# Scaling a pooled result run in two 16 KB halves instead of in one 32 KB piece

## The chip, the core and the metric

The kernel runs on one core of one Trainium2 chip. The metric is the device time of one execution in microseconds (us); less is better. The kernel before took 1569.69 us, the median of 3 runs (1565.55 to 1570.47).

## What is computed

The reference is an average pool over the last axis with window 4 and stride 4, so the windows do not overlap:

```python
x = randn(64, 256, 8192) in float32; kernel_size = stride = 4
for i in range(out_len):                      # out_len = 2048
    output[:, :, i] = mean(x[:, :, 4*i : 4*i + 4], axis=2)
```

Every output element is the sum of four neighbouring inputs, times 1/4. The input has 536.87 MB and the output 134.22 MB, and each byte crosses between HBM and SBUF once.

## The kernel before, in words

As a window never crosses a row, the whole input is treated as one long array. It is cut into 64 blocks of 128 partitions x 16384 floats (64 KB in each partition, 8 MB in all). Two consecutive blocks (k = 0 and k = 1) make a run, so there are 32 runs. A block gives 4096 results in each partition (16 KB), and a run gives 8192 (32 KB in each partition, 4 MB in all). There are two input buffers, `xt[0]` for every k = 0 block and `xt[1]` for every k = 1 block, and two result buffers, `ot[0]` and `ot[1]`, which alternate from run to run (`q`).

Four engines have fixed parts:

- SyncE (SP) issues the loads of 8 MB (`load`, line 63). It waits until VectorE has finished with a buffer (semaphore `free`, line 89) and at once issues the load of the next run's block into that buffer (`ahead`, line 92).
- VectorE (DVE) waits for a loaded block (`full[k]`, line 85), and ahead of a run's first block also for the store that last read this result buffer (`stored[q]`, line 87). Then it sums neighbours twice (`sums`): line 76 adds the even and odd elements of the block in place (16384 to 8192), and line 78 adds again into the half of `ot[q]` that belongs to the block (8192 to 4096).
- ScalarE (ACT) multiplies by 1/4 in place (line 95). SP tells it by the semaphore `summed` (line 91) that the sums are there.
- The store of 4 MB (line 97) is issued by ACT itself, after it has waited for its own multiplication (`scaled`). In the last run but one SP issues it, and waits for `scaled_last`.

The order of work is written out by hand with semaphores: `take(engine, sem, n)` (lines 59 to 60) makes an engine wait for a count and takes it off again, so all waits stand on line 60 in the profile. The function `pair` (lines 82 to 97) does one run. A loop of 15 iterations with two runs each covers runs 0 to 29 (line 119); run 30 stands by itself behind it (line 122) and issues the loads of the last run, whose k = 1 block is cut into two pieces (lines 112 to 113). Run 31 is written out in lines 126 to 141: it already scales its first half and its two quarter pieces separately, and ACT issues its stores of 3 MB and 1 MB.

Loads all go into SP's DMA queue, and the stores of runs 0 to 29 and 31 into ACT's. Both queues are served by the same 16 DMA engines.

Of the kernel before, what the change touches and what calls it, by code (L numbers as in the profile page):

```python
# [1 line left out]

# [4 lines left out]


FULL = 16384
PAIR = 2  # L10
ROUND = 2 * PAIR

TAIL = (8192, 8192)


@with_exitstack
def kernel(
    ctx: ExitStack,
    tc: tile.TileContext,
    x: bass.AP,  # L20
    kernel_size: bass.AP,
    stride: bass.AP,
    out: bass.AP,
):
    nc = tc.nc
    K, S = int(kernel_size), int(stride)
    assert K == S == 4
    B, C, L = x.shape
    assert L % K == 0
    P = nc.NUM_PARTITIONS  # L30
    dt = x.dtype
    add, mult = mybir.AluOpType.add, mybir.AluOpType.mult

    M = FULL // K
    blocks = B * C * L // P // FULL
    runs = blocks // PAIR
    assert blocks * P * FULL == B * C * L and blocks % ROUND == 0 and sum(TAIL) == FULL

    xr = x.rearrange("b c l -> (b c l)").rearrange("(n p k m) -> n k p m", p=P, k=PAIR, m=FULL)
    orun = out.rearrange("b c l -> (b c l)").rearrange("(n p m) -> n p m", p=P, m=PAIR * M)  # L40


    xt0 = ctx.enter_context(nc.sbuf_tensor([P, FULL], dt))
    xt1 = ctx.enter_context(nc.sbuf_tensor([P, FULL], dt))
    ot0 = ctx.enter_context(nc.sbuf_tensor([P, PAIR * M], dt))
    ot1 = ctx.enter_context(nc.sbuf_tensor([P, PAIR * M], dt))
    xt, ot = [xt0, xt1], [ot0, ot1]


    full = [nc.alloc_semaphore(f"full{k}") for k in range(2)]  # L50
    piece = [nc.alloc_semaphore(f"piece{k}") for k in range(len(TAIL))]
    free = nc.alloc_semaphore("free")
    summed = nc.alloc_semaphore("summed")
    summed_last = nc.alloc_semaphore("summed_last")
    scaled = nc.alloc_semaphore("scaled")
    scaled_last = nc.alloc_semaphore("scaled_last")
    stored = [nc.alloc_semaphore(f"stored{k}") for k in range(2)]

    def take(engine, sem, n):
        engine.wait_ge(sem, n).then_inc(sem, -n)  # L60

    def load(n, k):
        d = nc.sync.dma_start(out=xt[k][:, :], in_=xr[n, k])
        d.then_inc(full[k], 16)
        return d

    for k in range(2):
        tc.no_tile_sem_insts.add(load(0, k).ins.name)  # L70
    tc.close()
    tc.compile()  # L72

    def sums(t, o):
        w = t.shape[1]
        nc.vector.tensor_tensor(out=t[:, : w // 2], in0=t[:, ::2], in1=t[:, 1::2], op=add)  # L76
        nc.vector.drain()
        return nc.vector.tensor_tensor(  # L78
            out=o, in0=t[:, : w // 2 : 2], in1=t[:, 1 : w // 2 : 2], op=add
        )  # L80

    def pair(n, q, ahead, store):

        for k in range(PAIR):
            take(nc.vector, full[k], 16)
            if k == 0:
                take(nc.vector, stored[q], 16)
            sums(xt[k][:, :], ot[q][:, k * M : (k + 1) * M]).then_inc(free, 1)
            take(nc.sync, free, 1)
            if k == 1:  # L90
                nc.sync.sem_inc(summed, 1)
            ahead(k)
        done = scaled if store is nc.scalar else scaled_last
        take(nc.scalar, summed, 1)
        nc.scalar.mul(ot[q][:, :], ot[q][:, :], 1.0 / K).then_inc(done, 1)  # L95
        take(store, done, 1)
        store.dma_start(out=orun[n], in_=ot[q][:, :]).then_inc(stored[q], 16)


    zero = nc.const_aps.tensor(0.0, [P, 1], dt)  # L100
    nc.scalar.mul(ot[0][:, :1], zero, 1.0).then_inc(stored[0], 16)  # L101
    nc.scalar.sem_inc(stored[1], 16)

    edges = [sum(TAIL[:i]) for i in range(len(TAIL) + 1)]
    pieces = list(zip(edges[:-1], edges[1:]))
    xe, oe = xr[runs - 1, 1], orun[runs - 1]

    def ahead_of_last(k):
        if k == 0:
            load(runs - 1, 0)  # L110
        else:
            for sem, (a, b) in zip(piece, pieces):
                nc.sync.dma_start(out=xt[1][:, a:b], in_=xe[:, a:b]).then_inc(sem, 16)

    engines = (mybir.EngineType.SP, mybir.EngineType.DVE, mybir.EngineType.Activation)
    with nc.Fori(0, (runs - 2) // 2, 1, engines=engines) as r:
        for q in range(2):
            n = r * 2 + q
            pair(n, q, lambda k: load(n + 1, k), nc.scalar)


    pair(runs - 2, 0, ahead_of_last, nc.sync)

    take(nc.vector, stored[1], 16)
    take(nc.vector, full[0], 16)
    sums(xt[0][:, :], ot[1][:, :M]).then_inc(summed_last, 1)
    for k, (sem, (a, b)) in enumerate(zip(piece, pieces)):
        take(nc.vector, sem, 16)  # L130
        sums(xt[1][:, a:b], ot[1][:, M + a // K : M + b // K]).then_inc(summed_last, 1)
        if k == 0:
            take(nc.scalar, summed_last, 1)
            nc.scalar.mul(ot[1][:, :M], ot[1][:, :M], 1.0 / K)  # L134
        o = ot[1][:, M + a // K : M + b // K]
        take(nc.scalar, summed_last, 1)
        nc.scalar.mul(o, o, 1.0 / K).then_inc(scaled, 1)  # L137
        take(nc.scalar, scaled, 1)
        c = 0 if k == 0 else M + a // K
        d = M + b // K  # L140
        nc.scalar.dma_start(out=oe[:, c:d], in_=ot[1][:, c:d]).then_inc(stored[1], 16)
    take(nc.sync, stored[0], 16)
    take(nc.sync, stored[1], 16 * len(TAIL))


# [1 line left out]
_INS = ['x', 'kernel_size', 'stride']  # L147
_OUTS = [((64, 256, 2048), 'float32')]

_NUMBERS = {'kernel_size': 4, 'stride': 4}  # L150


# [26 lines left out]
```

## Time and profile before

| | |
|---|---|
| median of 3 runs | 1569.69 us |
| the profiled execution | 1568.75 us |
| its span, first to last instruction | 1567.4 us |
| VectorE busy | 839.8 us (54%) |
| ScalarE busy | 226.8 us (14%) |
| bytes through the DMA engines | 671.09 MB, 428 GB/s over the span |
| share of the 16 DMA engines' time, SP's queue q1 and ACT's queue q10 | 80.6% and 19.2% |
| one store of 4 MB from ACT, issue to landing | 33.5 us (median of 30) |
| one load of 8 MB, issue to landing | 35.2 us (median of 63) |

An engine counts as busy only while it computes; waits, semaphore steps and issuing a DMA do not count. A group of the profile stands for the instructions of one line, with their count, their busy time and the mean duration of one; the number behind the bar is the time the engine stood idle just before them, and what ended it. "DVEq L60" as the releaser is the engine's own wait in `take`. The timeline gives each instruction's start, measured from the start of the span.

### The profile page before, as it was taken

The page shows a single profiled execution, that of the slowest core. Times are in us where ns is not written, and L with a number is a line of the kernel's source. Part 1 is how long each engine was busy: PE and PEld are TensorE (multiplying, and loading weights), DVE is VectorE, ACT ScalarE, POOL GpSimd, SP SyncE. Part 2 cuts the span into 40 slices and gives each one's busy share as a digit, 9 for nine tenths or more (in the row PEclk, how much of TensorE's full clock was granted, in tenths as well). Part 3 has the DMA queues.
Part 4 walks back from the last instruction along what each step waited for, and adds up shares of the span by engine and source line. Part 5 has one row for each costly group of instructions (what it writes and reads, how often), then busy time and mean ns, then how long its engine had stood idle before and what let it go on. Part 6 is the DMA issues. An engine that isn't in the chain of part 4 may idle for free. (4 is left out here: it accounts for less than half of the span.)

```text
span 1567.4 us, 935 instructions
## 1 busy us (share of the span) xinstructions
DVE 839.8 (54%) x130; ACT 226.8 (14%) x36; POOL 0.2 (0%) x4
## 2 busy tenths in 40 slices
DVE  3654546545465454654546546465464654646546
ACT  0111011110111101111011110111101111011111
POOL 0000000000000000000000000000000000000000
DMA  9999999999999999999999999999999999999998
GB/s 428 415 428 442 428 421 435 430 426 440 422 439 426 445 426 429 437 420 439 428 426 431 427 436 428 429 426 431 433 423 428 423 427 434 428 429 424 431 429 378
DMA packets 14112, 671.09 MB, mean 428 GB/s; under 512 B 1568, under 2 KB 1568, under 8 KB 1568
## 3 DMA queue, kind: packets, MB, share of 16 engines
q1 hardware_dynamic: 9504, 541.07, 80.6%
q10 hardware_dynamic: 4608, 130.03, 19.2%
HBM read 536.87 MB, written 134.22 MB: 428 GB/s over the span
## 5 line engine op out<-in xcount | busy, mean ns | idle before, releaser
L76 DVE TENSOR_TENSOR xt<-xt 128x8192 f32<-128x8192 f32 (+1 forms) x65 | 556.5, 8561 | 710.2 <-DVEq L60 710.2
L95 ACT ACTIVATE ot<-ot 128x8192 f32<-128x8192 f32 x31 | 217.9, 7029 | 1306.3 <-ACTq L60 1306.3
L78 DVE TENSOR_TENSOR ot<-xt 128x4096 f32<-128x4096 f32 (+1 forms) x65 | 283.4, 4360 | 4.8
L134 ACT ACTIVATE ot<-ot 128x4096 f32<-128x4096 f32 x1 | 3.6, 3617 | 13.4 <-ACTq L60 13.4
L137 ACT ACTIVATE ot<-ot 128x2048 f32<-128x2048 f32 x2 | 3.8, 1910 | 8.0 <-ACTq L60 8.0
L101 ACT ACT_TABLE_LOAD x1 | 1.3, 1283 | 2.4 <-PEq L72 2.4
L101 ACT ACTIVATE ot<-const-float32-0.0 128x1 f32<-128x1 f32 x1 | 0.2, 202 | 0.0
L160 POOL MEMSET const-bfloat16-1.0<- 128x1 bf16 x1 | 0.1, 101 | 0.0
L160 POOL MEMSET const-uint8-127<- 128x1 uint8 x1 | 0.1, 101 | 0.0
L160 POOL MEMSET const-float32-0.0<- 128x1 f32 x1 | 0.1, 98 | 0.2 <-issue 0.2
L160 POOL MEMSET const-float32-1.0<- 128x1 f32 x1 | 0.1, 98 | 0.0
## 6 DMA issues: line engine op xcount, KB each, us to landing
out_dram<-ot ACTq DMA_DIRECT2D x30, 4096.0 KB, 33.5
xt<-in_x_dram SPq DMA_DIRECT2D x2, 4096.0 KB, 21.7
out_dram<-ot SPq DMA_DIRECT2D x1, 4096.0 KB, 32.2
out_dram<-ot ACTq DMA_DIRECT2D x1, 3072.0 KB, 12.5
out_dram<-ot ACTq DMA_DIRECT2D x1, 1024.0 KB, 10.4
xt<-in_x_dram SPq DMA_DIRECT2D x63, 35.2
```

The costliest lines, as they stand in the source:

```text
L76: nc.vector.tensor_tensor(out=t[:, : w // 2], in0=t[:, ::2], in1=t[:, 1::2], op=add)
L78: return nc.vector.tensor_tensor(out=o, in0=t[:, : w // 2 : 2], in1=t[:, 1 : w // 2 : 2], op=add)
L95: nc.scalar.mul(ot[q][:, :], ot[q][:, :], 1.0 / K).then_inc(done, 1)
L101: nc.scalar.mul(ot[0][:, :1], zero, 1.0).then_inc(stored[0], 16)
L134: nc.scalar.mul(ot[1][:, :M], ot[1][:, :M], 1.0 / K)
L137: nc.scalar.mul(o, o, 1.0 / K).then_inc(scaled, 1)
L160: nc = _bacc.Bacc("TRN2", target_bir_lowering=False, num_devices=1)
```

## The change

The multiplication by 1/4 moves into the loop over the two blocks. SP now increments `summed` after each block and not only after the second, ahead of the block's `ahead` load; ACT waits for one count of it and multiplies the 4096 results of that block. The second multiplication alone signals `done`, and the store of the whole 4 MB follows it as before. Nothing else is changed: the loads, the sums, the size and the number of the stores, and the last run (126 to 141) stay as they are.

```diff
             sums(xt[k][:, :], ot[q][:, k * M : (k + 1) * M]).then_inc(free, 1)
             take(nc.sync, free, 1)
-            if k == 1:
-                nc.sync.sem_inc(summed, 1)
+            nc.sync.sem_inc(summed, 1)
             ahead(k)
+            o = ot[q][:, k * M : (k + 1) * M]
+            take(nc.scalar, summed, 1)
+            means = nc.scalar.mul(o, o, 1.0 / K)
         done = scaled if store is nc.scalar else scaled_last
-        take(nc.scalar, summed, 1)
-        nc.scalar.mul(ot[q][:, :], ot[q][:, :], 1.0 / K).then_inc(done, 1)
+        means.then_inc(done, 1)
         take(store, done, 1)
         store.dma_start(out=orun[n], in_=ot[q][:, :]).then_inc(stored[q], 16)
```

On ACT, one multiplication of 128x8192 becomes two of 128x4096 in each of the 31 runs that `pair` does. On SP, one more semaphore increment stands ahead of each k = 0 load. The instructions of VectorE and their order are the same.

## Prediction

> **What bounds the kernel now.** I read the busy shares first. VectorE works 54% of the span and ScalarE 14%, so neither sets the time. The DMA line decides:
>
> ```profile
> DVE 839.8 (54%) x130; ACT 226.8 (14%) x36; POOL 0.2 (0%) x4
> ...
> DMA  9999999999999999999999999999999999999998
> GB/s 428 415 428 442 428 421 435 430 426 440 422 439 426 445 426 429 437 420 439 428 426 431 427 436 428 429 426 431 433 423 428 423 427 434 428 429 424 431 429 378
> ...
> q1 hardware_dynamic: 9504, 541.07, 80.6%
> q10 hardware_dynamic: 4608, 130.03, 19.2%
> ```
>
> All 16 DMA engines are 90% busy or more in every slice but the last, and the two queues together fill 80.6 + 19.2 = 99.8% of the engines' time. No 4 MB of store and no 8 MB of load goes away in this change, so the first question is only whether the engines can work faster or have holes to fill. The trace's packet records answer it. A row of a load is one packet of 64 KB, which took 2.418 us from the 10th to the 90th percentile; a row of a store (32 KB) took 1.213 us. At those durations, with each packet starting 4 ns before its predecessor's end as they do, all packets make 1546 us on each engine. Packets that are longer than that add 15.0 us an engine. The first packet starts 1.8 us into the span, and the rest of the 1567.4 is gaps and the tail. So the hole that any rearrangement can fill is about 15 us (1%), not more.
>
> Next I read the groups and one period of the timeline, for who waits.
>
> ```profile
> L76 DVE TENSOR_TENSOR xt<-xt 128x8192 f32<-128x8192 f32 x63 | 547.6, 8692 | 710.2 <-DVEq L60 710.2
> ...
> L95 ACT ACTIVATE ot<-ot 128x8192 f32<-128x8192 f32 x31 | 217.9, 7029 | 1306.3 <-ACTq L60 1306.3
> ...
> L134 ACT ACTIVATE ot<-ot 128x4096 f32<-128x4096 f32 x1 | 3.6, 3617 | 13.4 <-ACTq L60 13.4
> ```
>
> ```profile
> 724.55 8.69 DVE L76 TENSOR_TENSOR xt<-xt 128x8192 f32<-128x8192 f32 x1 [15.07 <-DVEq L60]
> 733.32 4.43 DVE L78 TENSOR_TENSOR ot<-xt 128x4096 f32<-128x4096 f32 x1
> 737.97 7.03 ACT L95 ACTIVATE ot<-ot 128x8192 f32<-128x8192 f32 x1 [41.89 <-ACTq L60]
> 745.20 8.69 DVE L76 TENSOR_TENSOR xt<-xt 128x8192 f32<-128x8192 f32 x1 [7.45 <-DVEq L60]
> 745.24 0.34 ACTq L97 DMA_DIRECT2D out_dram<-ot  x1
> 753.96 4.42 DVE L78 TENSOR_TENSOR ot<-xt 128x4096 f32<-128x4096 f32 x1
> 773.48 8.69 DVE L76 TENSOR_TENSOR xt<-xt 128x8192 f32<-128x8192 f32 x1 [15.09 <-DVEq L60]
> ```
>
> The reader is to see four things. VectorE waits ahead of both blocks of a run, 7.45 us ahead of k = 0 and about 15.1 us ahead of k = 1, and what it waits for is the load. A run takes 48.92 us (this group of rows comes back at 794.12, against 745.20). The next load stands in SP's queue within 0.3 us of the sums' end, so it is queued 7 or 15 us before the load ahead of it has landed: q1 never runs dry. And the store is issued 7.5 us after the sums' end (745.24 against 737.75), almost at the moment at which the k = 0 load lands.
>
> **The change part by part.**
>
> ACT's work. 31 multiplications of 7.029 us become 62 of 3.617 us (the row of line 134 has that shape): 217.9 us become 224.3, +6.4 us of busy time in all. What hides it is ACT's idle time, 41.9 us in each run. With that cover gone it would cost 0.2 us a run, 6.4 us.
> The Trainium skill states the same price against a split (ScalarE: Activation LUTs, section "What ACT_TABLE_LOAD costs"): an activation with immediate operands has a fixed 186 ns, which would be 5.8 us over 31 more of them as an estimate; the rows have 205 ns, and that is what I use.
>
> The path from sums to store. The half of k = 0 is scaled while VectorE waits for k = 1, off every path. After the second sums only 3.62 us of scaling are left where 7.03 were, so each of the 31 stores is issued 3.41 us sooner, at about 4.1 us behind the sums' end. Nothing is queued on ACT behind the new wait but the second multiplication and the store, and neither could start before.
>
> SP. One more increment stands ahead of each k = 0 load. The k = 1 load, which passes such an increment already, is issued 0.05 us later after its wait than the k = 0 load (0.28 against 0.23 us in the trace). That is 31 x 0.05 = 1.6 us if it lay on the path. It lies under the 15.1 us during which the load waits in the queue anyway: 0. In run 30 SP also waits for `scaled_last`; behind that stand only the final waits.
>
> What the earlier store does in the DMA engines. This is the only part that touches the bound. The engines alternate between the queues packet by packet: the records show load, store, load, store, 64 KB and 32 KB, as soon as ACT's queue holds something. A store's first packet follows 3.3 to 6.5 us behind its issue. On the engine that lands last, the k = 0 load now ends 0.3 us before the issue, two packets of the next load go first, and the store's eight packets follow in between the others, so that one of them is left when the k = 1 load is done. Moved 3.41 us forward, the store enters one load packet sooner, behind the first instead of the second packet of the k = 1 load. Its eighth packet then lies ahead of the k = 1 load's landing and no longer behind it: that load lands 1.21 us later, and the k = 0 load after it takes 1.21 us less from there. The two idle times of VectorE move by one store packet, 7.45 to about 6.2 us and 15.1 to about 16.3 us. Their sum and the period do not, since every engine still has 16 load and 8 store packets in a run: 0.
>
> The stall at a store's start. This is the unknown cost. Of the 15.0 us of longer packets, 12.6 lie within 9 us behind the issue of the 30 stores from ACT, mostly on the one packet ahead of a store's first: 0.42 us a store on an average engine. It is not constant: 1.02 us for the first store, which was issued 1.2 us after the load's landing; nothing for the second, which was issued 1.1 us before it; 0.04 to 0.84 for the others, all issued within 0.2 us of it. The profile does not show what makes it, and the change moves the issue relative to the landing, from 0 to some 2 us ahead. The bounds are therefore 0 a store, as in the second (-12.6 us), and 1.02, as in the first (30 x 0.60 = +18 us). I take 0.42, no change: 28 of the 30 rows lie between the ends with the same timing, so timing alone does not make it.
>
> Start and end. The first load's landing is untouched, and the first store (issued at 62.72) enters the same busy queues. At the end, SP's store of run 30 is issued at 1524.8 instead of 1528.17, but in q1 behind the two pieces issued at 1521 (landing up to 26.6 us later, 1548), so it moves nothing. The tail of run 31 is unchanged: its last store is issued at 1557.01 and lands 10.4 us later, at 1567.4, the end of the span.
>
> The sum is 0 + 0 + 0 on the profiled execution's 1568.75 us (span 1567.4 and 1.35 around it). The median of the runs shown lies 0.9 us above it; I predict between them, 1569.0 us.
>
> **The rivals.**
>
> 1. Slower: the stall grows. If the start of a store costs every engine what the first store's did, the 30 stores cost 18 us more: 1587 us. For it speaks that a single row shows this price on all 16 engines at once, and that the store now meets the end of one load and the start of another. Against it, the only row with an issue ahead of a landing shows none. It decides from 0.42 + 4.7/30 = 0.58 us a store on.
> 2. Faster: the stall goes, as in the second store: 1556 us. For it speaks that this row has an order most like the new one. Against it, it is one row, and several stores with the old timing (501.37, 598.95) had only 0.04 too. It decides below 0.27 us a store.
> 3. Slower: the store cuts into the k = 0 load and VectorE becomes late. One store packet ahead of the load's landing costs 1.21 us a run, 31 x 1.21 = 37 us if each run took it: 1606 us. It decides only if the k = 1 load is not in the queue by then; it is, 7.45 us early, six times that packet.
> 4. Faster: the early issue pays in full. If the 31 stores stood on the path, 31 x 3.41 = 106 us would go: 1463 us. Against it stands the 99.8% of the DMA engines and the 1546 us of packets alone, which forbid more than 1%. The Trainium skill's rule (DMA: Bandwidth & Descriptors, section "Rules for kernel authors") to issue a DMA early so that its fixed cost overlaps would argue for this rival; the trace has that cost already beside a full queue.
>
> That the change does not do what it says, with the store issued no sooner, would give the same time as the forecast; only the timeline tells it.
>
> **How the numbers follow.** A measurement of this kernel tells about 0.3% from no change, 4.7 us, so "same" is 1565.0 to 1574.4. No change that can be measured: 0.70. The stall grows: 0.14. The stall shrinks: 0.12. The store delays the loads beyond their cover: 0.03. The early issue pays: 0.01. So faster 0.13, same 0.70, slower 0.17. The unknown stall carries the range: 1556 with none of it, 1587 with the first store's. Together these hold well over 8 in 10.
>
> **What would show each step.** In the changed profile: 62 multiplications of 3.6 us at 224 us in all; stores issued about 4.1 us behind the sums' end; VectorE's idle times near 6.2 and 16.3 us; 80.6 and 19.2% for the queues; 48.9 us a run. What would make it wrong: a period that moves by more than 0.15 us (31 x 0.15 = 4.7), with longer packets around the store's start that add up to clearly more or less than 12.6 us an engine; or idle time on VectorE that shrinks in sum, which only shorter transfers could bring.

## The result and the profile after

The changed kernel is slower: 1581.39 us against 1569.69 (medians of 7 runs each), a ratio of 1.0078, 95% interval 1.0055 to 1.0101. Its profiled execution took 1578.58 us, with a span of 1577.3 us: 9.9 us more than before. It is the second quickest of the seven, so the profile shows a little less than the whole loss of the medians, 11.7 us.

The page of the changed kernel, in the order in which the page of before was read (busy shares, DMA, queues, groups):

```profile
DVE 839.8 (53%) x130; ACT 233.1 (15%) x67; POOL 0.2 (0%) x4
...
DMA  9999999999999999999999999999999999999999
GB/s 425 425 425 425 435 439 420 430 434 430 420 427 419 445 420 427 420 420 444 425 425 412 425 438 424 422 415 425 437 425 427 414 421 441 417 430 420 416 435 388
...
q1 hardware_dynamic: 9504, 541.07, 80.7%
q10 hardware_dynamic: 4608, 130.03, 19.1%
...
L76 DVE TENSOR_TENSOR xt<-xt 128x8192 f32<-128x8192 f32 (+1 forms) x65 | 556.5, 8561 | 720.1 <-DVEq L60 720.1
L94 ACT ACTIVATE ot<-ot 128x4096 f32<-128x4096 f32 x62 | 224.2, 3616 | 1307.6 <-ACTq L60 1307.6
```

The same packets, the same 99.8% of the engines' time, and yet 1577 us: the DMA engines are as full as before and move 425 GB/s, not 428. VectorE's work is the same to 0.1 us; its waiting for loads has grown by 9.9 us (720.1 against 710.2), the whole difference of the spans. ScalarE has its 62 multiplications of 3.6 us and waits no less. So nothing on an engine got slower; the transfers did. One run of the timeline of the changed kernel:

```profile
729.82 8.69 DVE L76 TENSOR_TENSOR xt<-xt 128x8192 f32<-128x8192 f32 x1 [16.39 <-DVEq L60]
738.58 4.42 DVE L78 TENSOR_TENSOR ot<-xt 128x4096 f32<-128x4096 f32 x1
743.22 3.62 ACT L94 ACTIVATE ot<-ot 128x4096 f32<-128x4096 f32 x1 [25.96 <-ACTq L60]
747.08 0.34 ACTq L98 DMA_DIRECT2D out_dram<-ot  x1
749.26 8.69 DVE L76 TENSOR_TENSOR xt<-xt 128x8192 f32<-128x8192 f32 x1 [6.26 <-DVEq L60]
```

The store is issued 4.08 us behind the sums' end (747.08 against 743.00), as the edit intended, and now 2.2 us ahead of the point at which VectorE takes up the k = 0 block (749.26); before, both came at once. From the third store to the thirtieth a run takes 49.25 us on average, against 48.89 before: 0.36 us more.

Where it went is read from the packet records, as in the prediction: the time by which packets are longer than their usual 2.418 or 1.213 us adds up to 25.2 us on an average engine, against 15.0. That is 10.2 us more, the difference of the spans to 0.3 us. The longer packets lie where they lay before, within 9 us behind a store's issue: 0.76 us for each store from the third on, against 0.42. I call this **the stall**; all values of it below are means of stores 3 to 30 unless they say otherwise.

### The profile page after: what moved, and what is told of

It is laid out like the page before. It is cut to its first block, busy times and chain, and to the rows that moved or that the text cites. A ratio compares the mean times of both kernels' runs of the same rounds, so it can differ in the third digit from the quotient of the medians.

```text
span 1577.3 us, 1028 instructions
## 1 busy us (share of the span) xinstructions
DVE 839.8 (53%) x130; ACT 233.1 (15%) x67; POOL 0.2 (0%) x4
## 3 DMA queue, kind: packets, MB, share of 16 engines
q1 hardware_dynamic: 9504, 541.07, 80.7%
q10 hardware_dynamic: 4608, 130.03, 19.1%
## 5 line engine op out<-in xcount | busy, mean ns | idle before, releaser
L76 DVE TENSOR_TENSOR xt<-xt 128x8192 f32<-128x8192 f32 (+1 forms) x65 | 556.5, 8561 | 720.1 <-DVEq L60 720.1
L94 ACT ACTIVATE ot<-ot 128x4096 f32<-128x4096 f32 x62 | 224.2, 3616 | 1307.6 <-ACTq L60 1307.6
L135 ACT ACTIVATE ot<-ot 128x4096 f32<-128x4096 f32 x1 | 3.6, 3617 | 15.6 <-ACTq L60 15.6
## 6 DMA issues: line engine op xcount, KB each, us to landing
out_dram<-ot ACTq DMA_DIRECT2D x1, 1024.0 KB, 10.4
```

What stands on the lines that cost most here:

```text
L94: means = nc.scalar.mul(o, o, 1.0 / K)
```

## The experiments

In every experiment the loads, sums and stores move the same bytes, unless the text says what is left out; "idle" multiplications work on a buffer of their own and only take time on ScalarE. `delay(times, n)` is so many idle multiplications of n elements, each waited for. Lines of other kernels than the changed one have other line numbers for the same statements.

**1. Is it the time of issue, or the split?** Two kernels take the change apart.

```diff
  # e1_late: the changed kernel, store 3.4 us later
+            if k == 1:
+                delay(1, 3600)
             means = nc.scalar.mul(o, o, 1.0 / K)
  # e2_one_half: the kernel before, one multiplication of half the run
-        nc.scalar.mul(ot[q][:, :], ot[q][:, :], 1.0 / K).then_inc(done, 1)
+        nc.scalar.mul(ot[q][:, M:], ot[q][:, M:], 1.0 / K).then_inc(done, 1)
```

> The changed kernel with one addition: between a run's first and second multiplication ScalarE does an idle multiplication of 3600 elements on a buffer of its own, so that the store is issued about 3.4 us later than in the changed kernel, as late as in the kernel before. Theory T (the time of issue against the landing of the k = 0 load sets the stall at a store's start): the stall falls back from 0.76 us to about 0.42 us a store and the time to that of the kernel before, within 4 us of 1569.7. Theory S (the split itself costs: more instructions on ScalarE, one more increment on SyncE ahead of a load): it stays slower by about 10 us, near 1580.

> The kernel before, with the one multiplication of a run cut to its second half, so that it takes 3.62 us; the first half of each run of runs 0 to 30 is left unscaled. The store is issued 3.4 us earlier, as in the changed kernel, but there is neither a second multiplication nor a further increment. Theory T: slower, near 1580 like the changed kernel, stall about 0.76 us a store. Theory S: no different from the kernel before, near 1570.

Measured: e1_late 1569.45 us, ratio to the kernel before 1.0000 (0.9990 to 1.0011), stall 0.42 us. e2_one_half 1575.71 us, 1.0059 (1.0034 to 1.0085), stall 0.70. With the whole split but the old time of issue nothing is lost; with the early issue and no split, more than half of the loss is there (6.4 us on the medians), and its interval overlaps that of the changed kernel. Theory T holds, theory S falls. The timeline of e1_late has the idle multiplication ahead of the real one of k = 1, and the store issued with the landing again:

```profile
738.12 3.20 ACT L66 ACTIVATE idle<-idle 128x3600 f32<-128x3600 f32 x1 [24.30 <-ACTq L62]
741.45 3.62 ACT L103 ACTIVATE ot<-ot 128x4096 f32<-128x4096 f32 x1
745.31 0.34 ACTq L107 DMA_DIRECT2D out_dram<-ot  x1
745.41 8.69 DVE L83 TENSOR_TENSOR xt<-xt 128x8192 f32<-128x8192 f32 x1 [7.51 <-DVEq L62]
```

**2. Another queue, and a later issue.**

```diff
  # e3_store_sp: the changed kernel, stores of the loop from SyncE
-            pair(n, q, lambda k: load(n + 1, k), nc.scalar)
+            pair(n, q, lambda k: load(n + 1, k), nc.sync)
  # e4_later (e8_plus2, e6_plus17, e7_plus22): the kernel before, store later
         take(nc.scalar, summed, 1)
+        delay(2, 3600)      # e8: (1, 1600)  e6: (5, 3600)  e7: (7, 3300)
         nc.scalar.mul(ot[q][:, :], ot[q][:, :], 1.0 / K).then_inc(done, 1)
```

> The changed kernel with all stores of the loop issued by SyncE into the queue of the loads (q1), where they stand between two loads and are not interleaved. Theory R (the stall comes when the empty queue q10 is started on all DMA engines beside a busy one): no longer packets at a store's start, 12 to 25 us less of them, time near 1556. Theory W (the stall comes from the first writes to HBM among reads, whichever queue): the longer packets stay and the time is within 1565 to 1582. VectorE's idle times should be near 6 us ahead of k = 1 and 16 us ahead of k = 0 in both.

> The kernel before, with the store issued 6.9 us later (two idle multiplications of 3600 elements ahead of the real one), so some 7 us behind the landing of the k = 0 load. Theory T predicts a change of the stall whose sign it does not know: if only an issue ahead of a landing is costly the stall falls to 0.42 us a store or less and the time is 1570 or less; if any distance from the landing is costly, 0.7 us or more and near 1580. Theory S: no different from the kernel before.

> The kernel before with one idle multiplication of 1600 elements: the store is issued about 1.8 us behind the landing of the k = 0 load, 9 us after the issue of the k = 1 load, and one load stands in q1. Theory L: between nothing and 0.42 us, 1553 to 1569 us. Theory D: about 0.3 us, near 1565. Theory Q: no stall, near 1553.

> The kernel before with five idle multiplications of 3600 elements ahead of the real one: the store is issued some 17 us after the landing of the k = 0 load, about 4 us after the issue of the next k = 0 load and 11 us ahead of the landing of the k = 1 load; two loads stand in q1. Theory L: no stall, 1553 to 1556 us. Theory D: stall about 0.76 us, near 1580. Theory Q: stall of 0.4 us or more, 1569 or more.

> The same with about 22 us of idle multiplications: the store is issued some 9 us after the issue of the next k = 0 load, 6 us ahead of the landing of the k = 1 load, again with two loads in q1. Theory L: little or no stall, 1553 to 1560 us. Theory D: stall about 0.3 us, near 1565. Theory Q: 0.4 us or more, 1569 or more.

| kernel | store's issue against the landing of a load | median us | ratio (95%) | stall us |
|---|---|---|---|---|
| changed | 2.2 ahead of k = 0 | 1581.39 | 1.0078 (1.0055 to 1.0101) | 0.76 |
| before | at k = 0 | 1569.69 | 1 | 0.42 |
| e8_plus2 | 0.5 or 1.7 behind k = 0, by turns | 1559.42 | 0.9940 (0.9919 to 0.9960) | 0.13 |
| e4_later | 4.3 behind k = 0 | 1553.32 | 0.9902 (0.9886 to 0.9919) | 0.00 |
| e6_plus17 | 11 ahead of k = 1 | 1553.07 | 0.9896 (0.9880 to 0.9913) | 0.00 |
| e7_plus22 | 6.1 ahead of k = 1 | 1553.31 | 0.9899 (0.9883 to 0.9916) | 0.00 |
| e3_store_sp | (in the loads' queue) | 1555.79 | 0.9919 (0.9902 to 0.9935) | 0.00 |

The distance is read from each timeline, as the time from the store's issue to the start of VectorE's sums on that block. In e4_later they are 4.30 us ahead of it:

```profile
737.24 7.03 ACT L103 ACTIVATE ot<-ot 128x8192 f32<-128x8192 f32 x1
740.21 8.69 DVE L83 TENSOR_TENSOR xt<-xt 128x8192 f32<-128x8192 f32 x1 [9.85 <-DVEq L62]
744.51 0.34 ACTq L105 DMA_DIRECT2D out_dram<-ot  x1
```

The stall falls from 0.76 us to nothing over 6.5 us of distance from the landing, and the time of the kernel with it. An issue 6.6 us later than in the kernel before is 1% faster, and an issue 3.4 us earlier is 0.8% slower. In e3_store_sp, where the 31 stores stand in q1 between two loads, there is no stall either, at the changed kernel's own time of issue. The page of e3_store_sp shows where the stores went:

```profile
q1 hardware_dynamic: 13824, 666.90, 99.3%
q10 hardware_dynamic: 288, 4.19, 0.6%
```

So theory W falls: writes among the reads do not stall by themselves. Theory R fits, but it is not shown alone: behind the load in q1 the store's first packets also come 28 to 31 us after its issue, against 3.4 to 7.7 us from q10 in the changed kernel. The run does not tell whether it is the second queue that stalls or the short time from issue to start. The Trainium skill (DMA: Bandwidth & Descriptors, section "Issuing engines are not separate DMA queues") says that DMAs of all issuing engines interleave on the same 16 engines, and that issuing from several saves only the sequencer's time. The interleaving is what the records show; the second part isn't all of it here, since the same stores from SyncE instead of ScalarE made 1555.79 us out of 1581.39.

**3. Is it VectorE's traffic?** The stalled packets fall together with the first addition of line 76 in the slow kernels, and not in the others. Three kernels test that.

```diff
  # e9_one_part: the changed kernel, sums on one partition
-            sums(xt[k][:, :], ot[q][:, k * M : (k + 1) * M]).then_inc(free, 1)
+            sums(xt[k][:1, :], ot[q][:1, k * M : (k + 1) * M]).then_inc(free, 1)
  # e10_sums_late: the changed kernel, first sums of a run behind the store's start
+                take(nc.vector, go, 1)            # ahead of the sums of k = 0
         store.dma_start(out=orun[n], in_=ot[q][:, :]).then_inc(stored[q], 16)
+        delay(2, 3600)
+        nc.scalar.sem_inc(go, 1)
  # e11_extra: store late as in e6, with idle VectorE work on it, ahead of the k = 0 load
+                for _ in range(4):
+                    nc.vector.drain()
+                    nc.vector.tensor_tensor(out=extra[:, :], in0=ot[1 - q][:, : M : 2], in1=ot[1 - q][:, 1 : M : 2], op=add)
```

> The changed kernel with the sums of runs 0 to 30 done on one partition instead of 128 (the same instructions and times on VectorE, 1/128 of its traffic; the other 127 partitions of those results are left unsummed). Theory V (what stalls the store's start is VectorE's first addition on the block that has just landed, which starts 2.2 us behind the issue in the changed kernel, at the issue in the kernel before, and is over or not begun in the runs without a stall): the stall goes, 1553 to 1556 us. Theory K (the cause lies in the DMA queues alone, near the change from one load to the next): stall stays near 0.76 us, about 1580 us.

> The changed kernel, but VectorE waits with the sums of a run's first block until about 7 us after the issue of the store of the run before, by when the store's first packets (3.3 to 6.7 us after the issue) are through; the load and the store keep their times. Theory V: no stall, 1553 to 1556 us. Theory K: about 0.76 us a store, near 1580.

> The kernel before with the store issued about 17 us later, as in e6_plus17, where there was no stall and VectorE was idle from 2.4 to 11 us after the issue; VectorE now does four additions of 2048 elements there on data that nobody needs. Theory V in its wide form (any VectorE work over all partitions during the store's start): stall 0.4 us or more, 1567 or more. Theory V in its narrow form (only the additions on a block that has just landed) and theory K: no stall, about 1553.

Measured: e9_one_part 1574.46 us, 1.0029 (1.0009 to 1.0050), stall 0.54; e10_sums_late 1576.93, 1.0047 (1.0029 to 1.0065), 0.59. In e10_sums_late VectorE does not begin until the store's first packets are through:

```profile
693.57 0.34 ACTq L107 DMA_DIRECT2D out_dram<-ot  x1
693.96 6.53 ACT L67 ACTIVATE idle<-idle 128x3600 f32<-128x3600 f32 x2 [0.62 <-ACTq L63]
700.75 8.69 DVE L84 TENSOR_TENSOR xt<-xt 128x8192 f32<-128x8192 f32 x1 [11.25 <-DVEq L63]
```

Its sums follow 7.18 us behind the issue, and most of the stall stays. e11_extra took 1561.43 us, 0.9947 (0.9930 to 0.9964), without a stall, though VectorE works while the store starts:

```profile
705.79 0.34 ACTq L113 DMA_DIRECT2D out_dram<-ot  x1
708.50 9.39 DVE L102 TENSOR_TENSOR extra<-ot 128x2048 f32<-128x2048 f32 x4
...
1527.03 0.34 SPq L113 DMA_DIRECT2D out_dram<-ot  x1
1527.12 8.69 DVE L85 TENSOR_TENSOR xt<-xt 128x8192 f32<-128x8192 f32 x1 [22.74 <-DVEq L64]
```

Its 8 us over e6_plus17 aren't in the runs, which take 48.30 us each. Most of them lie at the end: the wait for `go`, which keeps the extra work behind the store's issue, also holds the sums of the last run until the store of run 30 is issued. They begin at 1527.12, 10 us after their block landed, and the DMA engines run out of work before the last two stores are issued. Theory V falls. That the stall in e9 and e10 is smaller over the whole run comes from a late beginning: in both, the stall of the stores from the 3rd to the 6th is below 0.2 us, and over the last 12 it is 0.75 and 0.78 us, against 0.87 in the changed kernel. The beginning goes with the engines' spread, the time between the first and the last of the 16 DMA engines to finish one k = 0 load. In e9 the stores 3 to 8 stall by 0.07 us at most at a spread below 0.8 us, the last 12 at a spread of 2.7 to 3.5 us, with the load and nearly every store issued at the same distances throughout. Which of the two brings the other is open: the first larger stall of e9 (0.45 us, store 9) comes before the spread grows.

**4. Is it the landing, or a load that was only just issued?** In the changed kernel the k = 1 load is issued 3.8 us ahead of the store and 6 us ahead of the k = 0 load's end. Four kernels move that load.

```diff
  # e5_load_late: e1_late, and SyncE holds the k = 1 load for the idle multiplication
             nc.sync.sem_inc(summed, 1)
+            if k == 1:
+                take(nc.sync, go, 1)
             ahead(k)
...
                 delay(1, 3600)
+                nc.scalar.sem_inc(go, 1)
  # e13_early_load: the changed kernel, sums of half a block, idle work makes up for it
-            sums(xt[k][:, :], ot[q][:, k * M : (k + 1) * M]).then_inc(free, 1)
+            sums(xt[k][:, : FULL // 2], ot[q][:, k * M : k * M + M // 2]).then_inc(free, 1)
+            if k == 1:
+                delay(2, 3410)
  # e14_held_load: e13_early_load with the k = 1 load held back as in e5
  # e15_plus26: the kernel before with delay(8, 3420)
```

> As e1_late (store issued 3.4 us later than in the changed kernel, at the landing of the k = 0 load), but SyncE also waits for ScalarE's idle multiplication before it issues the next run's k = 1 load, so that this load is issued 3.8 us ahead of the store, as in the changed kernel, and not 7.2 us. Theory D (the stall follows the time between the last load's issue and the store's issue: 3.8 us cost 0.76 us, 7.2 us 0.42, 14.1 us nothing): stall about 0.76 us, near 1580 us. Theory L (it follows the distance from the landing of the load in flight: 2.2 us ahead costs 0.76, at it 0.42, 4.3 us behind nothing): about 0.42 us, near 1569. Theory Q (it comes when packets of two loads stand in q1 as the store's descriptors arrive): about 0.42 us, near 1569.

> The changed kernel with sums over half of each block in runs 0 to 30 (the other half of those results is left unsummed), so that VectorE is done 6.6 us sooner and the load behind is issued 6.6 us sooner; ScalarE makes up for it with 6.6 us of idle multiplication ahead of the second one, so that the store keeps its place 2.2 us ahead of the landing of the k = 0 load. The k = 1 load is then issued some 10 us ahead of the store and 12.6 us ahead of that landing. Theory F (the stall comes when the load that is about to begin, or has just begun, was issued only a few us before the store): little or no stall, 1553 to 1560 us. Theory L (only the distance from the landing counts): about 0.7 us a store, near 1578.

> As e13_early_load (half of the sums left out, the store 2.2 us ahead of the landing), but SyncE holds the k = 1 load back until the idle multiplications are over, so that it is issued 3.9 us ahead of the store and about 6 us ahead of the landing, as in the changed kernel. Theory F and theory L: about 0.7 us a store, near 1578 us, like the changed kernel. If it has no stall, the sums that are left out did it.

> The kernel before with the store issued some 26 us later: about 2 us ahead of the landing of the other load, k = 1, the same distance that the changed kernel has from the k = 0 load. The load that follows was issued 4 to 5 us ahead of the store and some 6 us ahead of that landing. Theory L and theory F: stall 0.5 us or more, 1570 or more. If only the change from a k = 0 to a k = 1 load can stall the store: no stall, near 1553.

| kernel | store, against the landing | next load, ahead of that landing | median us | ratio (95%) | stall us |
|---|---|---|---|---|---|
| e1_late | at k = 0 | 7.1 us | 1569.45 | 1.0000 (0.9990 to 1.0011) | 0.42 |
| e5_load_late | at k = 0 | 3.7 us | 1603.54 | 1.0226 (1.0200 to 1.0251) | 1.09 |
| e13_early_load | 2.2 ahead of k = 0 | 12.3 us | 1563.19 | 0.9982 (0.9960 to 1.0004) | 0.19 |
| e14_held_load | 2.2 ahead of k = 0 | 5.9 us | 1575.62 | 1.0046 (1.0025 to 1.0067) | 0.72 |
| e15_plus26 | 0 to 6 ahead of k = 1 | 2.3 to 7.8, median 5.7 us | 1586.26 | 1.0109 (1.0092 to 1.0126) | 0.69 |

The pair e13 and e14 has the same sums, the same idle work and the store at the same place; only the load behind it is issued 6.4 us earlier in the one. First e13_early_load, then e14_held_load:

```profile
1223.69 3.62 ACT L104 ACTIVATE ot<-ot 128x4096 f32<-128x4096 f32 x1
1227.55 0.34 ACTq L108 DMA_DIRECT2D out_dram<-ot  x1
1229.76 4.42 DVE L84 TENSOR_TENSOR xt<-xt 128x4096 f32<-128x4096 f32 x1 [12.62 <-DVEq L63]
```

```profile
1235.04 3.62 ACT L108 ACTIVATE ot<-ot 128x4096 f32<-128x4096 f32 x1 [0.20 <-ACTq L64]
1238.89 0.34 ACTq L112 DMA_DIRECT2D out_dram<-ot  x1
1241.06 4.42 DVE L85 TENSOR_TENSOR xt<-xt 128x4096 f32<-128x4096 f32 x1 [12.65 <-DVEq L64]
```

In both the store is 2.2 us ahead of the sums' start. In e13_early_load the stall of the last 12 stores is 0.01 us, in e14_held_load 0.78. So the distance from the landing alone isn't it (theory L in its pure form falls). That the early load did it is not shown by this pair. Over stores 3 to 8 both kernels stall alike, 0.57 and 0.58 us; in e13 the stall goes only while the spread grows from 0.6 us at the first store to 5.1 us, and in e14 the spread stays at 2.4 to 3.1 us over the last 12. The executions of e13 differ, too: they took 1559.67 to 1573.33 us, and the trace is of the quickest; those of e14 took 1572.36 to 1583.84.

For theory F, that a load issued only a few us before its turn is part of it, stands e5_load_late, at the old place of the store. Only the load is held back there, and the stall is 1.09 us against 0.42 in e1_late, from the beginning on (1.53 against 0.15 over stores 3 to 8):

```profile
707.33 17.52 SPq L71 DMA_DIRECT2D xt<-in_x_dram  x2
711.00 8.69 DVE L84 TENSOR_TENSOR xt<-xt 128x8192 f32<-128x8192 f32 x1 [7.44 <-DVEq L63]
711.03 0.34 ACTq L111 DMA_DIRECT2D out_dram<-ot  x1
```

Part of its 45 us of longer packets lies outside the stores' windows, so there the loads stall as well. e15_plus26 shows that a store near the k = 1 landing can stall too. Its distances vary from run to run, and its load was issued 0 to 6 us ahead of the store (median 1.9), so it carries less. Four of its stores (6, 16, 22 and 28) have the distances of the changed kernel, 2.2 us ahead of the landing and 3.5 us behind the load's issue, and stall by 0.12 to 0.26 us only. Against a plain theory F stands the first part of e13_early_load, where stores 3 to 12 still stalled by 0.19 to 0.95 us, and e7_plus22, where the next load was issued 0.95 us ahead of the store, and 7.1 us ahead of its turn, without a stall.

**5. The form without the stall and without idle work.**

```diff
  # e12_behind: each store is issued behind the next run's first multiplication
             means = nc.scalar.mul(o, o, 1.0 / K)
+            if k == 0 and behind is not None:
+                store_run(behind, 1 - q)          # take(nc.scalar, scaled, 1), then the dma_start
  # e16_behind_sp: the same, with the store of run 30 from SyncE as in the kernel before
```

> The changed kernel with the store of each run issued by ScalarE behind the next run's first multiplication, about 17 us after the landing of the k = 0 load, without any idle instruction. All theories that fit the runs so far expect almost no stall and 1553 to 1556 us; only if the idle multiplications themselves had removed it would it be 1565 or more.

> The form without a stall and without idle work: e12_behind (each store issued behind the next run's first multiplication), with the store of run 30 issued by SyncE behind the last loads as in the kernel before, so that it does not delay them. All theories: no stall and 1553 to 1555 us, some 3 us less than e12_behind.

Measured: e12_behind 1556.79 us, 0.9918 (0.9901 to 0.9935); e16_behind_sp 1553.11 us, 0.9897 (0.9880 to 0.9913), both with a stall of 0.00. e16_behind_sp leaves nothing out and beats both kernels, by 16 and by 28 us. In its timeline the store comes right behind the next k = 0 block's multiplication, 7 us ahead of the k = 1 landing:

```profile
699.62 4.42 DVE L78 TENSOR_TENSOR ot<-xt 128x4096 f32<-128x4096 f32 x1
704.27 3.62 ACT L98 ACTIVATE ot<-ot 128x4096 f32<-128x4096 f32 x1 [24.05 <-ACTq L60]
704.37 20.95 SPq L63 DMA_DIRECT2D xt<-in_x_dram  x2
704.50 0.34 ACTq L84 DMA_DIRECT2D out_dram<-ot  x1
711.49 8.69 DVE L76 TENSOR_TENSOR xt<-xt 128x8192 f32<-128x8192 f32 x1 [7.44 <-DVEq L60]
```

Here too a load is issued 0.13 us ahead of the store, and nothing stalls: its turn is 7 us away and the store's first packets are through by then. The page of e16_behind_sp:

```profile
span 1551.6 us, 1008 instructions
...
GB/s 414 443 414 433 433 446 422 441 441 434 424 446 433 433 433 420 445 433 433 433 431 434 433 433 433 435 434 444 434 424 446 422 447 433 421 444 424 441 429 409
```

A run takes 48.34 us, against 48.30 us of bare packets (16 x 2.414 + 8 x 1.2075 + three short ones). The longer packets sum to 1.7 us, of which 0.9 belong to the first store. Nothing is left in the middle of this kernel but its bytes.

## Why the prediction was wrong

Point by point, by its own steps:

- What bounds the kernel, and the most that can be won: right. The hole was put at about 15 us; the best kernels gained 16 us in the span (1551.6 against 1567.4).
- ScalarE's work: right, 224.2 us against 224.3, hidden as before; e1_late shows that it costs nothing.
- The time of issue: right, 4.08 us behind the sums' end against 4.1.
- The added increment on SyncE: right; e1_late has it and loses nothing.
- The order in the DMA engines: right. VectorE's waits are 6.26 and 16.39 us against 6.2 and 16.3 forecast. By itself this moves time from one wait to the other and costs nothing.
- The stall at a store's start: **wrong, and the whole error**. The step was "I take 0.42, no change". It was 0.76 from the third store on, and the 30 stores with some 22 us instead of 12.6 make more than 9 of the 9.9 us.
- The tail: right; the last store is issued at 1566.85, again 10.4 us ahead of the end of the span.

The forecast "no change" had a chance of 0.70 and rival 1, the growing stall, 0.14. Rival 1 was the right mechanism in the right place: past its point of 0.58 us a store, not as far as its end of 1.02, so 12 us and not 18 on the medians. That the range up to 1587 us holds the result is in part luck, since its upper end is the price of the first store. Rival 3 (VectorE late) never came near, its wait of 6.26 us stayed; rival 2 came true for a later issue, not for an earlier one.

Why the step failed can be said, too. The prediction let the first two stores stand for "behind" and "ahead of" a landing, and read the spread among the 28 others as a sign that timing doesn't set the stall. The first was wrong: the first store stalls by 0.76 to 1.19 us in most kernels here and the second not at all in most of them, whatever their time of issue, so these rows told of the start of a kernel and not of timing. The second is right as far as it goes, since timing alone doesn't make the stall (stores 3 to 27 of e9 have 0.01 to 1.07 us at one timing). But stalls that differ at one timing say nothing on how their mean moves when the timing does.

What is shown: the loss follows from the time of the store's issue (e1, e2 and the row of later issues); with the stores in the loads' queue it is gone (e3); VectorE's work near it isn't its cause (e9, e10, e11); and holding back the next load alone makes the stall larger (e5 against e1). What stays open: what a DMA engine does during the stall, whether the second queue by itself is needed for it, how the stall and the engines' spread hang together (e9, e10, e13), and whether the k = 1 landing has the same curve.

## What to carry to other kernels

When the DMA engines are 99.8% busy, an earlier issue can't be worth its lead; ask only what it will meet there. Look for packets that are longer than their kind, see which issue they follow, and move that issue into the middle of a long transfer, with the next transfer queued well ahead of its turn, or put it into the same queue: here 16 us in 1570 lay in that, and the change of 3.4 us in the other direction cost 12. A bound taken from the first rows of a run should be tried against rows from the middle.

## What was not expected

The 16 engines fall out of step. Their parts of one k = 0 load land within 0.6 us of each other in the first runs of the changed kernel, within 3.1 to 3.8 us in its last twenty; in e16_behind_sp they stay within 1.2 us. Being out of step isn't the cause by itself: the last stores of e13_early_load had 5.1 us of it and no stall, and the first store of the changed kernel stalls by 0.95 us at 0.6. But within the changed kernel, e9 and e10 the stall grows as the engines fall out of step.

Each store's start has a price on the 16 engines that changes with its place and with the next load's issue from nothing to 1.1 us on average, at the same bytes and the same busy share: the share of busy time counts a stalled packet as busy (80.7 and 19.1% in the changed kernel against 80.6 and 19.4% in e16_behind_sp), so it can't show such a loss.
